# Two-layer hybrid trunk on one core: wider column groups for the sparse attention's projections and the recurrence's values, four split weight pairs, a second set of banks for one FFN product

## The chip, the cores and the metric

The kernel runs on one core of a Trainium2 chip. The metric is the device time of one launch in microseconds (us). Three runs of the kernel before took 2005.44, 2006.55 and 2009.55 us; the median is 2006.55 us.

## The reference

The program is two layers of a decoder trunk for 512 tokens of width 1024, all in float32. The reference, cut to its lines that matter:

```python
h = rmsnorm(x, norm_mix)
(a_x, a_b, a_c, d_q, d_k, d_v, i_q, i_k, i_w,
 g_q, g_f, g_i, g_g, m_q, gate_logits) = split_cols(h @ w_in)
y_a = a_b * causal_conv3(a_c * a_x, conv_w)                 # A: gated convolution
# B: sparse attention: index scores, the 128 highest per token, softmax over these
rel = relu(einsum('bthd,bsd->bths', iq, ik) * idx_scale)
score = where(causal, einsum('bths,bth->bts', rel, iw), -inf)
_, sel = lax.top_k(score, topk)
p = softmax(where(valid, einsum('bthd,btkd->bthk', q, k[sel]) * att_scale, -inf))
y_b = einsum('bthk,btkd->bthd', p, v[sel])
o_c = hgrn2_chunkwise(silu(g_q), -expm1(log_f), g_i, log_f) # C: gated recurrence, values g_i
y_c = rmsnorm(o_c, hgrn_out_norm) * silu(g_g)
y_m = softmax(mq @ mk * scale) @ mv                         # M: attention into 256 memory tokens
merged = sum(gates[:, :, n] * (branches[n] @ w_lift[n]) for n in range(4))
x = x + merged @ w_out
hf = rmsnorm(x, norm_ffn)
gate, up = split(hf @ ffn_w_up, 2)
x = x + (silu(gate) * up) @ ffn_w_down
```

## The kernel before, in words

Every large product is done on TensorE in three float32 passes. An operand is split into a rounded part and a remainder (`_hi` and `_lo`), and `mm3` issues hi·hi, lo·hi and hi·lo for each 128-deep step of the contraction: lines L298, L299 and L300. A weight piece is loaded raw by SP's queue (L253; two raw buffers of 2048 columns), and split 1024 columns at a time: ScalarE writes `w_hi` (L118, the line of the helper through which all its operations go), VectorE writes `w_lo` (L262). A split pair is one such `w_hi` with its `w_lo`; there are `W_BUFS` = 3 of them, and a pair is free again when the last product has read it. `tc.high_priority(offset=AHEAD)` puts these splits ahead of other work.

With `features` the weight tile is what TensorE holds and h is streamed, always 512 columns. With `tokens` the h tile is held and the weights are streamed: the product is as wide as the piece of weights. `tokens` is used at two places:

- `projections` computes what sparse attention needs, for the columns of k, v, the index queries and key, and q: five pieces of 256, 256, 200, 256 and 256 columns, each of all eight contraction steps, and for each piece the four token tiles of 128. A handler (`c_kv`, `c_iq`, `c_last`, `c_q`) empties the accumulation bank: `unit` copies heads out with ScalarE, `headnorm` and `rope` follow, and `heads_T` transposes them.
- `values` computes the recurrence's values g_i as two pieces of 256 columns.

The order on each engine is made when the program is built: a list scheduler walks the instructions in the order of the code, with the priorities above, and keeps a modelled time. In the code, `script(EARLY[l], ...)` takes turns between four generators, by a string of letters: b is one piece of `projections`, c the convolution, m the memory branch, s a step of the top-k selection (8 highest by L881, replaced by L882, repeated). What is left of the selection is woven with `lift(3)` (the product of branch M with `w_lift`). Then `lift(0)` and `values` are woven with the attention itself, `attend`: per query tile and group of four heads, `dots` (L742, L743) into a bank `at`, an addition of the bias with a minimum on VectorE (L755, tile `prob`), the exponential, a reciprocal (L758) and the scaling, four transposes to a bank `tr` (L766), a copy `pt` by ScalarE, and the product with the values `vt` (L772). The recurrence follows. Its `logits` fill accumulation banks `mm` with `features`, and VectorE takes each of them out into a tile `zf`, `zq` or `zg` (L937). Those tiles take the memory of the attention's `prob` and `pt`. There are three banks `mm`, three `tr` and two `at`.

The memory branch reads its keys `mk` and values `mv` back from `kv`, an array in HBM that the start of the program writes; these loads (L664, L688) are in SP's queue between the loads of weights.

In the FFN seven products of blocks (`p1` to `p7`) form `A`, `B` and `C` in PSUM, and VectorE adds them up in tiles `merged` (`plus`, L1319). For the last column group q, `p4` accumulates anew in the banks `B`, after `plus(e, e, B)` has read them.

Of the kernel before, what the change touches and what calls it, by code (L numbers as in the profile page):

```python
# [41 lines left out]
NONC = -2.0e38  # L42
OFF = -1.0e30
AHEAD = 3000
EARLY = ["mmbcmmbmmbsccsmmcsssmsccbmb", "mmbmmbmmcbsccsmmcsssmsccbmb"]
MM_BUFS = 3
TR_BUFS = 3
AT_BUFS = 2
# [1 line left out]
HG = ["zzzHHlHlHzzzHHHHll", "zzzHHHHllzzzHHHllH"]  # L50
WARM, FILL = 9, 5
LOOK = ["0000", "0010"]
W_BUFS, RAW_BUFS, G_BUFS, PT_BUFS, PR_BUFS = 3, 2, 4, 2, 5
MV_BUFS, MP_BUFS = 1, 3
SPACER = 48
R1, R2 = 6, 3
# [14 lines left out]
def hybrid_trunk(ctx: ExitStack, tc: tile.TileContext, x, mem, positions, norm_mix, w_in, conv_w,  # L71
# [38 lines left out]
    def A(dst, src, func, **kw):  # L110
        names = tables.get(func, ())
        name = table["set"] if table["set"] in names else next(iter(names), None)
        if name is not None and name != table["set"]:
            load = act.preload_act_table_set(name)
            for u in table["users"]:
                tc.add_manual_dep(load.ins, u.name, order, reason="table set")
            table.update(set=name, load=load.ins, users=[])
        i = act.activation(dst, src, func, **kw)  # L118
        if name is not None:
            tc.add_manual_dep(i.ins, table["load"].name, order, reason="table set")  # L120
            table["users"].append(i.ins)
        return i

    def mm_ps():
        return bank["mm"]()
# [148 lines left out]
    def wchunk(src, kt, n):  # L274
        return Chunk(src, kt, n)

    def pair(a, k, s=slice(None)):
        return a[0][:, k, s], a[1][:, k, s]
# [8 lines left out]
                    mm3(ps, w.tile(k, j), pair(a, k0 + k), k0 + k == 0, k0 + k == kt - 1)  # L287
        return pss

    def tokens(w, a, t, ps, k0=0, kt=None):  # L290
        kt = w.kt if kt is None else kt
        for k in range(k0, k0 + w.kt):
            mm3(ps, pair(a, k, slice(t * P, (t + 1) * P)), w.at(k - k0), k == 0, k == kt - 1)

    def mm3(ps, a, b, first, last, go_on=False):
        ah, al = a
        bh, bl = b
        pe.matmul(ps, ah, bh, start=first, stop=False, skip_group_check=go_on)  # L298
        pe.matmul(ps, ah, bl, start=False, stop=False, skip_group_check=go_on)  # L299
        pe.matmul(ps, al, bh, start=False, stop=last, skip_group_check=go_on)  # L300
# [249 lines left out]
    def mixer(l, h, norms, cm, cf):  # L550
# [171 lines left out]
                        yield  # L722

        def values(hv):
            for q in range(2):
                w = wchunk(w_in[l][:, C_GI + q * 256:C_GI + (q + 1) * 256], KD, 256)
                for t in range(NT):
                    ps = mm_ps()[:, :256]
                    tokens(w, h, t, ps)
                    A(hv[:, t, q * 256:(q + 1) * 256], ps, AF.Copy, scale=r_t[:, t:t + 1])  # L730
                yield

        with pool_("dsa") as dp:
            qS = dp.tile([P, 8, S], F32R, name="qS")
# [45 lines left out]
            with pool_("idx") as ip:  # L780
# [39 lines left out]
                def unit(ps, t, c0, heads):  # L820
                    u = ip.tile([P, 4, HD], F32, name="unit", bufs=3)[:, :heads]
                    A(u.rearrange("p a b -> p (a b)"), ps[:, c0:c0 + heads * HD], AF.Copy, scale=r_t[:, t:t + 1])
                    return u
# [11 lines left out]
                    A(dst[0][:, s], ps, AF.Copy)  # L835
                    dve.tensor_sub(dst[1][0:HD, s], ps[0:HD], f(dst[0][0:HD, s]))

                def iq_part(ps, t, c0, heads, h0):
                    u = unit(ps, t, c0, heads)
                    rope(u, heads, t)  # L840
                    heads_T(iqS, h0, u.rearrange("p a b -> p (a b)"), heads, t)

                def c_kv(ps, t):
                    A(vt[:, t, :], ps[:, 64:128], AF.Copy, scale=r_t[:, t:t + 1])
                    twin(ps, t, 0, True, kS)
                    iq_part(ps, t, 128, 2, 0)

                def c_iq(ps, t):
                    iq_part(ps, t, 0, 4, 2)

                def c_last(ps, t):
                    A(iw[:, t, :], ps[:, 192:200], AF.Copy, scale=r8_t[:, t:t + 1])
                    iq_part(ps, t, 0, 2, 6)
                    twin(ps, t, 128, False, ikS)

                def c_q(q):
                    def go(ps, t):
                        u = unit(ps, t, 0, 4)
# [3 lines left out]
                    return go  # L862

                def select(t):
                    n = (t + 1) * P
# [19 lines left out]
                    dve.tensor_scalar(biases[t], score, REPL, OFF, op0=OP.not_equal, op1=OP.mult)  # L885

                def projections():
                    for c0, n, handle in ((C_DK, 256, c_kv), (C_DK + 256, 256, c_iq), (C_DK + 512, 200, c_last),
                                          (C_DQ, 256, c_q(0)), (C_DQ + 256, 256, c_q(1))):
                        w = wchunk(w_in[l][:, c0:c0 + n], KD, n)  # L890
                        for t in range(NT):
                            ps = mm_ps()[:, :n]
                            tokens(w, h, t, ps)
                            handle(ps, t)
                        yield

# [284 lines left out]
    def ffn(l, h, sx, ssq, xr, spare, late):  # L1181
# [9 lines left out]
        with tc.tile_pool(name="ffn", bufs=1) as fp:  # L1191
# [44 lines left out]
            def accs(name):  # L1236
                return [bank[name]() for _ in range(2)]
# [14 lines left out]
            def p5(q):  # L1252
                d = st[q]
                d["C"] = accs("C")
                product(d["C"], S1, d["X"].split(), True)
# [26 lines left out]
                product(st[q]["B"], S3, st[q]["Y"].split(), False)  # L1282

            def p4(q):
                product(st[q]["B"], A22, st[q]["X"].split(), False)

            def silu_mul(dst, src, t, other):
                A(dst, src, AF.Silu, scale=norm["r"][:, t:t + 1])
# [33 lines left out]
            for q in range(Q):  # L1322
                n = widths[q]
                d1, e, u, g = (tmps(i, n) for i in ((0, 1, 2, 3) if q % 2 else (3, 1, 2, 0)))
                p1(q, flush)
                d = st[q]
                if q == 0:
                    p5(0)
                    late()
                    r = norm_token(ssq)  # L1330
                    nr = small(NT, name="nrstd_t", bufs=2)
                    dve.tensor_scalar(nr, r, -1.0, None, op0=OP.mult)
                    norm.update(r=r, n=nr)
                with hi_prio():
                    for t in range(2):
                        A(d1[t], d["A"][t][:, :n], AF.Copy)
                plus(e, d1, d["C"], n)
                p6(q)
                plus(u, d1, d["B"], n)
                p3(q)  # L1340
                if q + 1 < Q:
                    first_sum(q + 1)
                plus(u, u, d["C"], n)
                p2(q)
                for t in range(2):
                    silu_mul(g[t], d["A"][t][:, :n], t, u[t])
                p7(q)
                plus(e, e, d["B"], n)
                turn(g, 0, q)
                if q + 1 < Q:  # L1350
                    p5(q + 1)
                p4(q)
                plus(d1, d1, d["B"], n)
                for t in range(2):
                    silu_mul(d1[t], d1[t], t + 2, e[t])
                pending.append((d1, 2, q))
                if q in ends:
                    flush()
                    res = down(q)
# [40 lines left out]
```

## Time and profile before

| what | value |
|---|---|
| median of three runs | 2006.55 us |
| the profiled execution's own time | 2013.66 us |
| its span, first to last instruction | 2012.0 us |
| TensorE matmuls (PE), busy share of the span | 99% |
| TensorE weight loads (PEld) | 84% |
| VectorE (DVE) | 69% |
| ScalarE (ACT) | 51% |
| mean granted TensorE clock | 0.997 |

The profile is of one execution; the span leaves out 1.66 us before the first and after the last instruction. The busy share of an engine is an average over all stages. A duration in the timeline is that of one instruction from its start to its modelled end; TensorE overlaps consecutive matmuls, so that the time which one adds is the distance between two starts. The idle time in front of an instruction stands in brackets, with what ended it.

### The profile page before, as it was taken

How to read it: one execution, taken by the hardware profiler on the slowest of the kernel's cores; microseconds unless marked ns; L12 is line 12 of the kernel's file. 1: busy time of each engine (PE TensorE's matmuls, PEld its weight loads, DVE VectorE, ACT ScalarE, POOL GpSimd, SP SyncE). 2: the span in 40 equal slices, each digit the busy share in tenths (PEclk: the TensorE clock that was granted, in tenths of full speed). 3: DMA queues.
4: the chain of work that ended last, by engine and by line, in shares of the span. 5: the costliest groups of instructions: out<-in, count | busy, mean ns of one | idle time of the engine just before them, and what ended most of it. 6: DMA issues, size and time to landing. Idle time of an engine off the chain costs nothing. (4 is left out here: it accounts for less than half of the span.)

```text
span 2012.0 us, 26848 instructions
## 1 busy us (share of the span) xinstructions
PE 1999.4 (99%) x10249; PEld 1685.9 (84%) x10249; DVE 1391.2 (69%) x2649; ACT 1034.6 (51%) x1797; POOL 69.6 (3%) x85
## 2 busy tenths in 40 slices
PE   9999999999999999999999999999999999999999
PEld 7898988888888888888889898878888888888887
DVE  6679998547666788458657889853687577863772
ACT  7554543766564655325445455366666455532551
POOL 1000000000000010000000000000000000100100
PEclk9999999999999999999999999999999999999999
DMA  8623233222224376354342313331222446644442
GB/s 280 198 82 105 69 95 95 63 64 84 84 84 147 105 199 168 105 136 105 110 157 90 95 58 95 95 95 42 86 83 73 136 122 172 167 126 126 107 113 94
DMA packets 174548, 226.89 MB, mean 113 GB/s; under 512 B 5954, under 2 KB 124308, under 8 KB 174420
## 3 DMA queue, kind: packets, MB, share of 16 engines
q1 hardware_dynamic: 157120, 193.55, 30.3%
q0 software_dynamic: 13344, 23.21, 7.0%
q10 hardware_dynamic: 3956, 8.42, 1.1%
q8 instruction: 81, 1.33, 0.3%
q14 instruction: 47, 0.39, 0.1%
HBM read 214.67 MB, written 10.49 MB: 112 GB/s over the span
## 5 line engine op out<-in xcount | busy, mean ns | idle before, releaser
L118 ACT ACTIVATE w_hi<-w_raw 128x1024 fp32r<-128x1024 f32 (+1 forms) x362 | 373.4, 1033 | 470.7 <-PE mm L299 153.4
L262 DVE TENSOR_TENSOR w_lo<-w_raw,w_hi 128x1024 fp32r<-128x1024 f32 x258 | 311.9, 1210 | 216.2 <-ACT w_hi L118 210.5
L298 PE MATMUL mm<-h_hi,w_hi 128*128 128x512 f32 x960 | 378.8, 396 | 0.6 <-ACT w_hi L118 0.6
L299 PE MATMUL mm<-h_lo,w_hi 128*128 128x512 f32 x960 | 376.8, 393 | 0.0
L300 PE MATMUL mm<-h_hi,w_lo 128*128 128x512 f32 x960 | 374.3, 391 | 0.0
L298 PEld LDWEIGHTS mm<-h_hi,w_hi 128*128 128x128 f32 x960 | 180.4, 188 | 38.0 <-issue 1.7
L300 PEld LDWEIGHTS mm<-h_hi,w_lo 128*128 128x128 f32 x960 | 180.4, 188 | 36.9 <-issue 0.5
L299 PEld LDWEIGHTS mm<-h_lo,w_hi 128*128 128x128 f32 x960 | 180.5, 188 | 36.6 <-issue 1.4
L1177 DVE TENSOR_TENSOR w_lo<-w_raw,w_hi 128x1024 fp32r<-128x1024 f32 (+1 forms) x104 | 117.9, 1142 | 52.6 <-ACT w_hi L118 52.4
L299 PE MATMUL mm<-w_lo,h_hi 128*128 128x256 f32 (+1 forms) x448 | 128.9, 288 | 0.0
L300 PE MATMUL mm<-w_hi,h_lo 128*128 128x256 f32 (+1 forms) x448 | 128.6, 287 | 0.0
L298 PE MATMUL mm<-w_hi,h_hi 128*128 128x256 f32 (+1 forms) x448 | 127.4, 286 | 0.0
L300 PE MATMUL mm<-y_hi,w_lo 128*128 128x512 f32 x256 | 101.3, 396 | 0.0
L299 PE MATMUL mm<-y_lo,w_hi 128*128 128x512 f32 x256 | 100.5, 393 | 0.0
L298 PE MATMUL mm<-y_hi,w_hi 128*128 128x512 f32 x256 | 100.2, 393 | 0.0
L118 ACT ACTIVATE w_hi<-f_raw 128x1024 fp32r<-128x1024 f32 (+1 forms) x64 | 62.7, 979 | 66.4 <-PE B L300 38.6
L299 PEld LDWEIGHTS mm<-w_lo,h_hi 128*128 128x128 f32 x448 | 86.6, 193 | 2.2 <-issue 1.5
L300 PEld LDWEIGHTS mm<-w_hi,h_lo 128*128 128x128 f32 x448 | 86.6, 193 | 1.4 <-issue 0.8
L298 PEld LDWEIGHTS mm<-w_hi,h_hi 128*128 128x128 f32 x448 | 86.3, 194 | 0.5
L118 ACT ACTIVATE prob<-prob,small 128x128 f32<-128x128 f32 (+3 forms) x128 | 69.0, 556 | 32.1 <-DVE small L755 25.0
L1177 DVE TENSOR_TENSOR w_lo<-f_raw,w_hi 128x1024 fp32r<-128x1024 f32 (+1 forms) x64 | 71.7, 1122 | 17.1 <-ACT w_hi L118 17.0
L299 PE MATMUL B<-w_lo,s_hi 128*128 128x512 f32 (+1 forms) x192 | 71.7, 375 | 0.2 <-DVE w_lo L1177 0.2
(438 smaller groups left out, 4350.3 us busy)
## 6 DMA issues: line engine op xcount, KB each, us to landing
w_raw<-in_w_in_dram SPq DMA_DIRECT2D x72, 1024.0 KB, 5.2
w_raw<-in_ffn_w_up_dram SPq DMA_DIRECT2D x60, 512.0 KB, 4.8
w_raw<-in_ffn_w_down_dram SPq DMA_DIRECT2D x18, 1024.0 KB, 5.4
w_raw<-in_w_lift_dram SPq DMA_DIRECT2D x32, 512.0 KB, 3.4
w_raw<-in_ffn_w_up_dram POOLq DMA_DIRECT2D x24, 512.0 KB, 6.3
f_raw<-in_ffn_w_up_dram SPq DMA_DIRECT2D x20, 512.0 KB, 5.0
w_raw<-in_w_out_dram SPq DMA_DIRECT2D x8, 1024.0 KB, 5.3
f_raw<-in_ffn_w_up_dram POOLq DMA_DIRECT2D x16, 512.0 KB, 8.6
```

The costliest lines, as they stand in the source:

```text
L118: i = act.activation(dst, src, func, **kw)
L262: dve.tensor_sub(lo, raw[:, k:e], f(hi))
L298: pe.matmul(ps, ah, bh, start=first, stop=False, skip_group_check=go_on)
L299: pe.matmul(ps, ah, bl, start=False, stop=False, skip_group_check=go_on)
L300: pe.matmul(ps, al, bh, start=False, stop=last, skip_group_check=go_on)
L1177: dve.tensor_sub(lo, self.raw[:, 2 * i:2 * i + 2, :], f(hi))
```

## The change

`projections` takes its columns in three groups of 512, 200 and 512, and `values` in one of 512. A new function `halves` loads a group of 512 as two raw pieces of four contraction steps each, which are four split pairs; `tokens` walks over both pieces for one token tile before it goes to the next. `W_BUFS` becomes 4, and the memory for the fourth pair comes from a smaller scratch for DMA descriptors (`dynamic_dma_scratch_size=4096`). The handlers first copy all heads out of the bank, and then go on with them. The strings `EARLY` have three b instead of five. In the FFN the last `p4` accumulates in banks `C`, and `plus` for the earlier content of `B` stands ahead of it.

```diff
-EARLY = ["mmbcmmbmmbsccsmmcsssmsccbmb", "mmbmmbmmcbsccsmmcsssmsccbmb"]
+EARLY = ["mmbcmmmmbsccsmmcsssmsccbm", "mmbmmmmcbsccsmmcsssmsccbm"]
-W_BUFS, RAW_BUFS, G_BUFS, PT_BUFS, PR_BUFS = 3, 2, 4, 2, 5
+W_BUFS, RAW_BUFS, G_BUFS, PT_BUFS, PR_BUFS = 4, 2, 4, 2, 5
-    def tokens(w, a, t, ps, k0=0, kt=None):
-        kt = w.kt if kt is None else kt
-        for k in range(k0, k0 + w.kt):
-            mm3(ps, pair(a, k, slice(t * P, (t + 1) * P)), w.at(k - k0), k == 0, k == kt - 1)
+    def halves(src, n):
+        per = min(KD, 2048 // n)
+        return [(k0, wchunk(src[k0 * P:(k0 + per) * P], per, n)) for k0 in range(0, KD, per)]
+
+    def tokens(ws, a, t, ps):
+        for k0, w in ws:
+            for k in range(k0, k0 + w.kt):
+                mm3(ps, pair(a, k, slice(t * P, (t + 1) * P)), w.at(k - k0), k == 0, k == KD - 1)
         def values(hv):
-            for q in range(2):
-                w = wchunk(w_in[l][:, C_GI + q * 256:C_GI + (q + 1) * 256], KD, 256)
-                for t in range(NT):
-                    ps = mm_ps()[:, :256]
-                    tokens(w, h, t, ps)
-                    A(hv[:, t, q * 256:(q + 1) * 256], ps, AF.Copy, scale=r_t[:, t:t + 1])
-                yield
+            ws = halves(w_in[l][:, C_GI:C_GI + 512], 512)
+            for t in range(NT):
+                ps = mm_ps()
+                tokens(ws, h, t, ps)
+                A(hv[:, t, :], ps, AF.Copy, scale=r_t[:, t:t + 1])
+            yield
                 def c_kv(ps, t):
                     A(vt[:, t, :], ps[:, 64:128], AF.Copy, scale=r_t[:, t:t + 1])
+                    u0, u1 = unit(ps, t, 128, 2), unit(ps, t, 256, 4)
                     twin(ps, t, 0, True, kS)
-                    iq_part(ps, t, 128, 2, 0)
+                    iq_part(u0, t, 0)
+                    iq_part(u1, t, 2)
...
-                    for c0, n, handle in ((C_DK, 256, c_kv), (C_DK + 256, 256, c_iq), (C_DK + 512, 200, c_last),
-                                          (C_DQ, 256, c_q(0)), (C_DQ + 256, 256, c_q(1))):
-                        w = wchunk(w_in[l][:, c0:c0 + n], KD, n)
+                    for c0, n, handle in ((C_DK, 512, c_kv), (C_DK + 512, 200, c_last), (C_DQ, 512, c_q)):
+                        ws = halves(w_in[l][:, c0:c0 + n], n)
             def p4(q):
-                product(st[q]["B"], A22, st[q]["X"].split(), False)
+                d = st[q]
+                if q == Q - 1:
+                    d["C"] = accs("C")
+                product(d["BC"[q == Q - 1]], A22, d["X"].split(), q == Q - 1)
...
+                if q + 1 == Q:
+                    plus(d1, d1, d["B"], n)
                 p4(q)
-                plus(d1, d1, d["B"], n)
+                plus(d1, d1, d["BC"[q + 1 == Q]], n)
...
-    nc = _bacc.Bacc("TRN2", target_bir_lowering=False, num_devices=1)
+    nc = _bacc.Bacc("TRN2", target_bir_lowering=False, num_devices=1, dynamic_dma_scratch_size=4096)
```

Three places where the order moves are shown. The first is SP's queue at the first piece of `projections` in layer 0. `w_raw` are pieces of weights (8x256 is a piece of eight contraction steps of 256 columns), `mk` and `mv` the keys and values read back from `kv0`. Before:

```order
L253 DMA w_raw_973<-in_w_in_dram 128x8x256
L253 DMA w_raw_1253<-in_w_in_dram 128x8x256
L253 DMA w_raw_1391<-in_w_in_dram 128x8x256
L664 DMA mk_837<-kv0 128x512
L664 DMA mk_839<-kv0 128x512
L688 DMA mv_935<-kv0 128x512
```

The same place after the change:

```order
L253 DMA w_raw_973<-in_w_in_dram 128x4x512
L253 DMA w_raw_983<-in_w_in_dram 128x4x512
L253 DMA w_raw_1323<-in_w_in_dram 128x8x256
L253 DMA w_raw_1497<-in_w_in_dram 128x8x256
L668 DMA mk_837<-kv0 128x512
L668 DMA mk_839<-kv0 128x512
```

One more load of weights stands in front of the first `mk`, and the first wide group is two loads.

The second place is TensorE at the end of layer 0's attention: `tr<-ident,prob` are transposes of the probabilities, `tr<-pt,vt` products with the values, `mm<-w,h` belong to `values` (h held), and `mm<-h,w` to the recurrence's `logits`. Before, the last products of the attention stand among both:

```order
L298 MATMUL mm<-w_hi,h_hi 128x256
L766 MATMUL tr<-ident,prob 128x128 x4
L772 MATMUL tr<-pt,vt 64x256 x6
L299 MATMUL mm<-w_lo,h_hi 128x256
L300 MATMUL mm<-w_hi,h_lo 128x256
L298 MATMUL mm<-w_hi,h_hi 128x256
L299 MATMUL mm<-w_lo,h_hi 128x256
L300 MATMUL mm<-w_hi,h_lo 128x256
L298 MATMUL mm<-h_hi,w_hi 128x512
L299 MATMUL mm<-h_lo,w_hi 128x512
L300 MATMUL mm<-h_hi,w_lo 128x512
```

After the change:

```order
L769 MATMUL tr<-ident,prob 128x128
L745 MATMUL at<-k_hi,qS 128x512
L746 MATMUL at<-k_lo,qS 128x512
L775 MATMUL tr<-pt,vt 64x256 x2
L769 MATMUL tr<-ident,prob 128x128 x15
L775 MATMUL tr<-pt,vt 64x256 x8
L302 MATMUL mm<-h_hi,w_hi 128x512
L303 MATMUL mm<-h_lo,w_hi 128x512
L304 MATMUL mm<-h_hi,w_lo 128x512
```

From the last `dots` (L745, L746) to the end of the attention no product of another branch stands between; before there were 73 matmuls of `values` and `logits` between the same `dots` and the attention's last two products.

The third place is VectorE there, after the change, with the buffer numbers: `mm_4454`, `mm_4455` and `mm_4518` are the three accumulation banks, filled by `logits` ahead of the rows above, and the row L302 above is the first of a fourth bank's worth.

```order
L758 ISA prob_4161,small_4162<-at_4158,bias3_809 128x512
L758 ISA small_4162 128x1
L780 TENSOR_TENSOR y_lo_3378<-tr_4117,y_hi_3377 128x2x128
L761 RECIPROCAL small_4163<-small_4163 128x1
L938 TENSOR_TENSOR zf_4504<-mm_4454,rstd_521 128x512
L938 TENSOR_TENSOR zf_4506<-mm_4455,rstd_521 128x512
L938 TENSOR_TENSOR zq_4568<-mm_4518,rstd_521 128x512
```

All three banks are emptied behind the attention's last reciprocal, the first by the row `zf_4504`, which writes into memory that the attention's `prob` and `pt` had. Before, the matmuls of `values` stood in that stretch, and their banks are emptied into a tile with memory of its own.

## Rows read from the trace of the kernel before

**Rows 1.** The page's first part: busy time, share of the span, instructions.
```profile
PE 1999.4 (99%) x10249; PEld 1685.9 (84%) x10249; DVE 1391.2 (69%) x2649; ACT 1034.6 (51%) x1797; POOL 69.6 (3%) x85
```
**Rows 2.** The waits of TensorE: line, releaser, total us, times, longest us.
```profile
PE at L298 <- DMA mk<-kv: 2.0, 1, 2.0
PE mm L298 <- ACT w_hi L118: 1.7, 2, 1.1
...
PE B L298 <- DVE merged L1319: 1.0, 2, 0.5
```
**Rows 3.** Groups by shape on PE: count, busy us, mean ns, idle before.
```profile
L299 PE MATMUL mm<-w_lo,h_hi 128*128 128x256 f32 x384 | 111.2, 290 | 0.0
L300 PE MATMUL mm<-w_hi,h_lo 128*128 128x256 f32 x384 | 110.7, 289 | 0.0
L298 PE MATMUL mm<-w_hi,h_hi 128*128 128x256 f32 x384 | 109.7, 288 | 0.0
```
**Rows 4.** Timeline of PE, 256 columns: start us, duration us, instruction.
```profile
92.01 0.28 PE L298 MATMUL mm<-w_hi,h_hi 128*128 128x256 f32 x1
...
94.53 0.28 PE L298 MATMUL mm<-w_hi,h_hi 128*128 128x256 f32 x1
```
**Rows 5.** Timeline of PE, 512 columns, in the FFN of layer 0.
```profile
859.92 0.39 PE L298 MATMUL A<-a_hi,w_hi 128*128 128x512 f32 x1
...
865.82 0.39 PE L300 MATMUL A<-a_hi,w_lo 128*128 128x512 f32 x1
```
**Rows 6.** Timeline of PE at the first product with the memory's keys.
```profile
78.84 1.05 PE L677 MATMUL tr<-ones_h,sq 128*128 128x1 f32 x8 [0.33 <-ACT sq L118]
81.86 0.38 PE L298 MATMUL at<-mk,qg_hi 128*128 128x256 f32 x1 [1.96 <-DMA mk<-kv]
```
**Rows 7.** Windows behind it: busy us (count) of each engine, granted clock, DMA.
```profile
83.40:90.20 6.80, 6.80 (x34) 6.80 (x33) 1.72 (x10) 3.03 (x13) 0.52 (x1) 0.51 0.05 18
90.20:94.60 4.40, 4.40 (x39) 4.40 (x38) 2.41 (x17) 3.02 (x12) 0.00 (x0) 1.00 0.00 0
```
**Rows 8.** Timeline of SP's DMA issues there.
```profile
73.41 0.37 SPq L253 DMA_DIRECT2D w_raw<-in_w_in_dram  x1
74.00 1.86 SPq L664 DMA_DIRECT2D mk<-kv  x2
```
**Rows 9.** Timeline of DVE there: the split that frees the slot.
```profile
76.12 1.23 DVE L262 TENSOR_TENSOR w_lo<-w_raw,w_hi 128x1024 fp32r<-128x1024 f32 x1 [1.02 <-ACT w_hi L118]
```
**Rows 10.** Timeline of PE at the last p4 of layers 0 and 1.
```profile
978.24 0.36 PE L298 MATMUL B<-w_hi,h_hi 128*128 128x256 f32 x1 [0.52 <-DVE merged L1319]
...
1950.27 0.36 PE L298 MATMUL B<-w_hi,h_hi 128*128 128x256 f32 x1 [0.52 <-DVE merged L1319]
```
**Rows 11.** The page's fifth part, the weight splits on ACT and DVE.
```profile
L118 ACT ACTIVATE w_hi<-w_raw 128x1024 fp32r<-128x1024 f32 (+1 forms) x362 | 373.4, 1033 | 470.7 <-PE mm L299 153.4
L262 DVE TENSOR_TENSOR w_lo<-w_raw,w_hi 128x1024 fp32r<-128x1024 f32 x258 | 311.9, 1210 | 216.2 <-ACT w_hi L118 210.5
```
**Rows 12.** Windows of layer 0's selection and attention, columns as in rows 7.
```profile
150.00:200.00 50.00, 50.00 (x241) 41.73 (x240) 45.32 (x109) 21.16 (x43) 0.21 (x2) 1.00 0.34 106
...
400.00:450.00 50.00, 50.00 (x327) 41.84 (x326) 19.48 (x40) 30.77 (x57) 1.49 (x4) 1.00 0.21 64
```
**Rows 13.** Timeline of PE, the last attention group of layer 0.
```profile
420.19 0.50 PE L742 MATMUL at<-k_hi,qS 128*128 128x512 f32 x1
...
429.00 0.60 PE L766 MATMUL tr<-ident,prob 128*128 128x128 f32 x4
429.53 1.52 PE L772 MATMUL tr<-pt,vt 128*64 128x256 f32 x12
```
**Rows 14.** Timeline of ACT, the same group.
```profile
422.73 0.72 ACT L118 ACTIVATE prob<-prob,small 128x512 f32<-128x512 f32 x1 [0.23 <-DVE small L758]
...
426.11 1.57 ACT L118 ACTIVATE pt<-tr 128x512 f32<-128x512 f32 x3 [2.29 <-PE tr L766]
```
**Rows 15.** Timeline of DVE, the first bank of logits.
```profile
440.87 0.69 DVE L937 TENSOR_TENSOR zf<-mm,rstd 128x512 f32<-128x512 f32 x1 [0.63 <-PE mm L300]
```

More of the change, by code (lines that the diff above doesn't have):

```diff
@@ L836, in twin, with iq_part @@
                     dve.tensor_sub(dst[1][0:HD, s], ps[0:HD], f(dst[0][0:HD, s]))
-                def iq_part(ps, t, c0, heads, h0):
-                    u = unit(ps, t, c0, heads)
+                def iq_part(u, t, h0):
+                    heads = u.shape[1]
                     rope(u, heads, t)
@@ L844, in c_kv, with c_q @@
                     A(vt[:, t, :], ps[:, 64:128], AF.Copy, scale=r_t[:, t:t + 1])
+                    u0, u1 = unit(ps, t, 128, 2), unit(ps, t, 256, 4)
                     twin(ps, t, 0, True, kS)
-                    iq_part(ps, t, 128, 2, 0)
-                def c_iq(ps, t):
-                    iq_part(ps, t, 0, 4, 2)
+                    iq_part(u0, t, 0)
+                    iq_part(u1, t, 2)
                 def c_last(ps, t):
                     A(iw[:, t, :], ps[:, 192:200], AF.Copy, scale=r8_t[:, t:t + 1])
-                    iq_part(ps, t, 0, 2, 6)
+                    u0 = unit(ps, t, 0, 2)
                     twin(ps, t, 128, False, ikS)
-                def c_q(q):
-                    def go(ps, t):
-                        u = unit(ps, t, 0, 4)
+                    iq_part(u0, t, 6)
+                def c_q(ps, t):
+                    us = [unit(ps, t, q * 256, 4) for q in range(2)]
+                    for q, u in enumerate(us):
                         headnorm(u, 4, gq_b[l])
@@ L861, in go @@
                         heads_T(qS, 4 * q, u.rearrange("p a b -> p (a b)"), 4, t)
-                    return go
                 def select(t):
@@ L887, in projections @@
                 def projections():
-                    for c0, n, handle in ((C_DK, 256, c_kv), (C_DK + 256, 256, c_iq), (C_DK + 512, 200, c_last),
-                                          (C_DQ, 256, c_q(0)), (C_DQ + 256, 256, c_q(1))):
-                        w = wchunk(w_in[l][:, c0:c0 + n], KD, n)
+                    for c0, n, handle in ((C_DK, 512, c_kv), (C_DK + 512, 200, c_last), (C_DQ, 512, c_q)):
+                        ws = halves(w_in[l][:, c0:c0 + n], n)
                         for t in range(NT):
                             ps = mm_ps()[:, :n]
-                            tokens(w, h, t, ps)
+                            tokens(ws, h, t, ps)
                             handle(ps, t)
```

## The prediction

> **What bounds the kernel now.** I read the page's first part before anything else: TensorE is busy for 99% of the span, VectorE for 69%, ScalarE for 51% [rows 1]. Then the waits of TensorE, to see whether the 1% is worth having: the longest is 2.0 us, before the first product with the memory's keys, and the two before the last `p4` add up to 1.0 us; what else there is stays under 2 us a line [rows 2]. So the kernel is a dense stream of matmuls, and the time changes in three ways only: by what a matmul costs, by a wait that goes, by a wait that comes. For the third I went through the order of the changed program on TensorE and looked for places where it has nothing else to do, then priced these from the timeline of before. All sums are made against the profiled execution, 2013.66 us (span 2012.0 and 1.66 around it), and carried over to the median of the runs, 2006.55, by adding the same difference.
>
> **Width.** The pieces that become 512 wide are 1152 matmuls of 256 columns over both layers (three lines of 384, [rows 3]): per layer 4 of the 5 pieces of projections and both of the values, 6 pieces x 4 token tiles x 8 steps x 3 passes = 576. They become 576 of 512 columns. The mean of 290 ns in rows 3 is not their price, since neighbours overlap; the distance of starts is. From 92.01 to 94.53 there are 21 steps in 2.52 us: 120 ns [rows 4]. From 859.92 to 865.82 there are 26 steps in 5.90 us: 227 ns [rows 5]. So 1152 x 0.120 = 138.2 us become 576 x 0.227 = 130.8 us: **-7.5 us**. All of it is on the path, as PE is what bounds. The piece of 200 columns stays.
>
> The Trainium skill ("TensorE: Matmul & The Clock Gate", section "Back-to-back issue gap") gives N/2.4 + 2.5 ns for an isolated matmul of N columns at the fast clock; it says itself that this leaves out the weight loads at small N. By that formula a pair of 256 would cost 218.4 ns against 215.8, and the change would be worth 576 x 2.6 ns = 1.5 us. The trace differs, 240 against 227, and the measurement decides.
>
> **The last `p4`.** It has banks of its own, so the wait of 0.52 us in each layer goes [rows 10]; the matmul behind the gap also takes longer to get going (0.36 us where its neighbours take 0.28), which makes about 0.6 us each: **-1.2 us**. The additional `plus` ahead of it lies on VectorE beside p4's matmuls. Bounds: 0 (the banks C come as late) to -1.4.
>
> **The start.** TensorE waits 1.96 us for `mk`, after a stretch of eight matmuls of one column [rows 6], and then runs 6.80 us with a granted clock of 0.51 before it is back at 1.00 [rows 7]: at 0.51 that stretch does 3.5 us of work, so it loses about 3.3 us. Together 5.3 us hang on this load. It was issued at 74.00 [rows 8] and landed at 81.86. In the changed order one more load of weights stands in SP's queue ahead of it, and that one waits for a raw buffer, that is for the split which before stood at 76.12 and ended at 77.35 [rows 9]. So `mk` is issued at about 78.0 and lands 7.9 us later, at 85.9. TensorE also comes later: ahead of the product the new order has 43 matmuls of the projections' first group, 512 wide, 43 x 0.227 = 9.8 us, where 24 of 256 stood, 2.9 us. It came there at 79.90 (81.86 less the wait), so now 6.9 us later, at 86.8, or a little before, since one matmul of another kind has moved behind it. That is less than 1 us after the load. If it waits 2 us again nothing is gained, if it doesn't wait 5.3 are. I take **-3.5**, two thirds of the way to no wait, for a lead of under 1 us is not safe.
>
> **The splits.** A group of 512 wants four pairs for its first token tile. A pair is a ScalarE split of 1.03 us and a VectorE split of 1.21 us [rows 11], which overlap. The first pair of the next group is free when the last token tile has done its first two steps, 18 matmuls x 0.227 = 4.1 us ahead of the group's end, and needs 2.2 us; the fourth is free only at the group's end, and is wanted 18 x 0.227 = 4.1 us later against the same 2.2. So there are 1.9 us in hand each time, as long as the splits aren't queued behind other work; VectorE is 45.32 of 50 us busy during the selection [rows 12], but the splits have priority over it. I take 0; the other end is 1 us for each of six groups, +6. The handlers' copies move from one bank of 256 to one of 512 with the same work: 0.
>
> **The attention's end.** Here something comes. VectorE bounds the selection [rows 12], so the attention doesn't move up with TensorE's work: in the new order more of `lift(0)` and of the values stands ahead of the first `dots`, and less is left beside the last ones. Behind the last `dots` of a layer before there are 73 matmuls of values and logits; now there are only transposes (15) and products with `vt` (10), and then a logits matmul whose bank must first be emptied by `zf`. That VectorE operation stands behind the attention, for its memory is that of `prob` and `pt`. So TensorE runs through the attention's chain with empty hands:
>
> Last `dots` at 0 (before: 420.19, [rows 13]); minimum, exponential and reciprocal until the scaling starts at 2.54, which ends at 3.26 (before: 422.73 and 0.72 us, [rows 14]). Then the transposes, 0.3 to the first bank; four copies `pt` on ScalarE, of which three took 1.57 us [rows 14], so 2.1; the last products, 0.13 each (12 in 1.52 us, [rows 13]) and the hop to VectorE, 0.4 together; `zf`, 0.69 [rows 15]; the next matmul. That makes 6.9 us. TensorE's own work in it is 0.5 for the dots, 15 transposes at 0.11 (four are 0.60 from the first start to the last end [rows 13], which is three steps and a last duration much like the 0.28 of rows 4) and 10 products at 0.13, together 3.4 us. So it is idle for 3.5 us; if ScalarE still has two scalings of neighbouring heads (0.72 each) in front, 4.9. I take 4.5 in each of two layers: **+9 us**. In the trace of before the same chain took from 420.19 to beyond 429.53, and no row of the waits has it, because the values' matmuls covered it.
>
> **The sum:** -7.5 - 1.2 - 3.5 + 9.0 = -3.2, so 2010.5 in the profile and 2003.4 in the median; I say 2003.5.
>
> **The rivals.**
>
> 1. *The tails are covered.* TensorE reaches the attention's end later than I think (it runs the real order with waits that I can't see), so that `zf` is through when it is wanted; for it speaks that before shows no wait on any operation of the attention, although its transposes stood just as close behind their copies. Against it, the order has no filler there. Then -7.5 - 1.2 - 3.5 = -12.2, and with half a wait left in one layer -10: 1994.5 to 1997.
>
> 2. *The clock falls at the tails: slower.* The only long gap of the trace, 1.96 us, was followed by 6.80 us at 0.51 [rows 6, 7], 1.2 instead of 2.4 GHz. The tails' gaps are longer, with transposes and short products between them. If the clock falls after each of them, at 3.3 us apiece, and the wait is 5.0 each, the tails cost 16.6 instead of 9.0: -12.2 + 16.6 = +4.4, 2011.0. It decides as soon as a tail's wait exceeds the 1.96 us by which the clock fell at the start and stays unbroken; for one tail alone it is +0.1 to +0.6, 2007. Against it: the waits are split into pieces by transposes and products.
>
> 3. *The width is worth only its columns.* If the 120 ns of rows 4 hold only where I read them and elsewhere a 256 costs half a 512, 113.5 ns [rows 5], the first term is 0 and the time 2011; with the skill's formula it is 2009.5. Against it: the same 0.28 and 0.29 us of duration in rows 3 over all 1152.
>
> 4. *Splits of four pairs are late*, one us for each of six groups: +2.8, 2009.4.
>
> 5. *The change doesn't do what it says*: `p4` waits for the banks C instead and `mk` is as late as before: 3.5 + 1.2 are not gained, 2008.
>
> **Chances.** Forecast as summed, with its own range of 2001 to 2006: 0.40. Rival 1: 0.22. Rival 2 with both tails 0.10, with one tail 0.10. Rival 3: 0.03, rival 4: 0.08, rival 5: 0.07. What a measurement of this kernel can tell from no change is 0.2%, 4.0 us: faster is below 2002.5, slower above 2010.6. Faster: all of rival 1, and of the forecast the two fifths in which the start gains its full 5.3 or the tails cost 3.5: 0.22 + 0.16 = 0.38. Slower: of rival 2 with both tails and of rival 3 about two thirds, and a part of rivals 4 and 5 together with a lost start, 0.09 + 0.08 = 0.17. Within: 0.45. The range for 8 in 10 cuts rival 1's best tenth and the worst of rival 2: 1995 to 2012.
>
> **What would show it.** Right: the distance of starts 0.227 us in projections and values; no row of the waits for `merged` L1319 at p4; two waits of TensorE of 3 to 5 us in total at the end of the attention, around 415 to 430 and 1355 to 1370 us, on `zf`, on ScalarE's `pt` or on `prob`; in the windows behind them a granted clock of 1.00. Wrong: PE idle in the projections on `w_hi` or `w_lo` (rival 4), a window at 0.5 behind the attention (rival 2), no wait there at all (rival 1), and `mk` with 2 us again (part of rival 5). The forecast fails above all if the tail's chain is hidden, or is much longer than 5 us a layer.

## The result and the profile after

The changed kernel takes 2026.78 us (four runs, 2024.76 to 2028.42), the kernel before beside it 2007.72 us: a ratio of 1.0095, 95% interval 1.0078 to 1.0113. It is 19.1 us slower. The prediction said 2003.5 us, with a range of 1995 to 2012, and gave slower a chance of 0.17. It was wrong.

The profiled execution took 2027.79 us, 14.1 more than that of before. The two figures differ because the profiled run of before (2013.66) is one of its longer ones: it has the wait for `mk` and the half clock behind it [rows 6, 7], some 5.5 us together, and a kernel with the same start has less of it (0.2 us of wait in the one with `p4` alone, below). So the medians are explained with the start left out.

The first part of the page after the change, which answers to [rows 1]:

```profile
PE 1998.3 (99%) x9673; PEld 1654.5 (82%) x9673; DVE 1389.4 (69%) x2653; ACT 1029.6 (51%) x1789; POOL 69.9 (3%) x85
```

TensorE is busy for 1.1 us less, not 7.5, and its idle time has grown from 12.6 to 27.7 us. The mean granted clock is 0.997 in both, so it is not half clock that takes the rest of the 7.5; the busy time counts late starts without a gap too, and the *excess* below holds both. The waits of TensorE (line, releaser, total, times, longest) answer to [rows 2]. `gate` is the tile into which VectorE empties a bank of `lift`'s gates; `mprob` are the memory branch's probabilities, `mpt_hi` the copy of their transposes, `qg_hi` and `qg_lo` the two parts of its queries.

```profile
PE mm L302 <- DVE gate L575: 6.4, 4, 2.4
PE mm L302 <- DVE qg_lo L678: 3.2, 3, 1.6
PE at L302 <- ACT mpt_hi L118: 2.6, 2, 1.4
PE C L302 <- DVE merged L1323: 2.0, 2, 1.6
PE tr L769 <- ACT prob L118: 1.9, 4, 0.6
PE mm L302 <- DVE zf L938: 1.7, 2, 0.9
```

None of the first four is in the list of before, and of the six only the last two groups (`prob`, `zf`) are at the place that the prediction named.

**What came as forecast.** The width: one group of the three of `tokens` (count, busy, mean ns, as in [rows 3]), and the timeline of a wide group, first and last of 18 starts without a gap:

```profile
L303 PE MATMUL mm<-w_lo,h_hi 128*128 128x512 f32 x192 | 75.1, 393 | 0.0
```

```profile
90.10 0.39 PE L302 MATMUL mm<-w_hi,h_hi 128*128 128x512 f32 x1
...
93.96 0.39 PE L304 MATMUL mm<-w_hi,h_lo 128*128 128x512 f32 x1
```

17 steps in 3.86 us are 0.227 each, and three lines of 192 are the 576. The start: SP's issue of `mk`, TensorE's first product with it, and the granted clock behind that (columns as in [rows 7]) answer to [rows 6 to 8]:

```profile
77.04 1.52 SPq L668 DMA_DIRECT2D mk<-kv  x2
```

```profile
85.29 0.95 PE L681 MATMUL tr<-ones_h,sq 128*128 128x1 f32 x8
86.10 0.37 PE L302 MATMUL at<-mk,qg_hi 128*128 128x256 f32 x1
```

```profile
86.00:90.00 4.00, 4.00 (x23) 3.47 (x23) 1.36 (x8) 2.54 (x10) 0.00 (x0) 1.00 0.00 0
```

`mk` goes out 3.0 us later and the product starts 4.2 us later, without a wait, and the clock stays at 1.00.

**What was not forecast: the memory branch.** Beside the projections, TensorE stops in both layers. First the windows of TensorE, before and after (busy, count, granted clock, DMA), then its timeline, that of ScalarE, and a window of all engines (busy of PE, PEld, DVE, ACT, POOL, granted clock, DMA), all three after:

```profile
100.00:150.00 50.00, 50.00 (x356) 1.00 0.29 87
100.00:150.00 50.00, 47.31 (x280) 0.97 0.38 117
```

```profile
138.11 0.70 PE L714 MATMUL tr<-ident,mprob 128*128 128x128 f32 x4 [0.33 <-DVE mprob L712]
140.06 0.58 PE L302 MATMUL at<-mpt_hi,mv 128*128 128x256 f32 x1 [1.25 <-ACT mpt_hi L118]
...
143.76 0.50 PE L302 MATMUL mm<-h_hi,w_hi 128*128 128x512 f32 x1 [0.77 <-DVE qg_lo L678]
```

```profile
137.37 2.00 ACT L118 ACTIVATE w_hi<-w_raw 128x1024 fp32r<-128x1024 f32 x2
139.26 0.26 ACT L118 ACTIVATE iw<-mm,r_t 128x8 f32<-128x8 f32 x1
139.41 0.59 ACT L118 ACTIVATE mpt_hi<-tr 128x512 fp32r<-128x512 f32 x1
```

```profile
137.00:144.00 7.00, 4.65 (x24) 3.89 (x24) 5.65 (x10) 5.16 (x12) 0.00 (x0) 0.76 0.40 118
```

The chain probabilities, transposes, copy, product with `mv` has nothing between its steps any more; the copy `mpt_hi` stands behind two weight splits on ScalarE, and TensorE waits through it, and then runs at the lower of its two levels, 1.2 GHz (granted clock 0.50 from 140.2 to 143.4 us, 0.76 over the window). In layer 1 the same comes at 1117 to 1122 us, at full clock, and one more wait before it. A window of PE, then PE, ACT and DVE at that earlier wait:

```profile
1080.00:1124.00 44.00, 39.95 (x244) 1.00 0.40 124
```

```profile
1087.13 0.50 PE L302 MATMUL mm<-h_hi,w_hi 128*128 128x512 f32 x1 [1.61 <-DVE qg_lo L678]
```

```profile
1085.11 0.69 ACT L118 ACTIVATE qg_hi<-mm,prm 128x512 fp32r<-128x512 f32 x1 [4.79 <-PE mm L304]
...
1086.49 0.47 ACT L118 ACTIVATE unit<-mm,rstd_t 128x256 f32<-128x256 f32 x1
```

```profile
1086.32 0.75 DVE L678 SCALAR_TENSOR_TENSOR qg_lo<-mm,prm,qg_hi 128x512 fp32r<-128x512 f32 x1 [3.15 <-ACT sq L118]
```

ScalarE's order has `qg_hi` ahead of the `unit` copies of a wide tile; it sits idle 4.79 us for `qg_hi`'s bank, and the `unit` copies behind it come after it. No run shows whether they could have come sooner: their buffers are read by transposes that start at 1085.02.

**What was not forecast: the selection.** At the wide q group TensorE first waits for a rotated unit and then for a bank that VectorE has not emptied; PE, then DVE:

```profile
257.88 0.41 PE L814 MATMUL tr<-ident,unit 128*128 128x128 f32 x2 [0.28 <-DVE unit L799]
260.69 0.50 PE L302 MATMUL mm<-h_hi,w_hi 128*128 128x512 f32 x1 [2.40 <-DVE gate L575]
```

```profile
257.65 0.42 DVE L808 TENSOR_TENSOR unit<-unit,small 128x256 f32<-128x256 f32 x1
257.99 0.55 DVE L883 MAX8 m<-score 128x8 f32<-128x384 f32 x1
...
259.08 0.43 DVE L809 TENSOR_TENSOR unit<-unit,gq 128x256 f32<-128x256 f32 x1
...
259.95 0.68 DVE L575 TENSOR_TENSOR gate<-mm,rstd 128x512 f32<-128x512 f32 x1
```

VectorE has no gap there, while TensorE does 20.25 us in a window of 24 (columns: busy, count, granted clock, DMA). Before, it had no gap there; its window stands first:

```profile
250.00:300.00 50.00, 50.00 (x227) 1.00 0.29 89
250.00:274.00 24.00, 20.25 (x96) 1.00 0.20 65
```

The bank is emptied by `gate` at 259.95, behind q's normalization and the selection.

**The attention's end**, as forecast in kind; PE and then DVE, which answer to [rows 13, 15]:

```profile
446.46 0.55 PE L769 MATMUL tr<-ident,prob 128*128 128x128 f32 x3 [0.64 <-ACT prob L118]
447.48 1.12 PE L769 MATMUL tr<-ident,prob 128*128 128x128 f32 x4 [0.47 <-ACT pt L118]
448.53 2.99 PE L775 MATMUL tr<-pt,vt 128*64 128x256 f32 x16
452.38 0.50 PE L302 MATMUL mm<-h_hi,w_hi 128*128 128x512 f32 x1 [0.87 <-DVE zf L938]
```

```profile
451.64 1.29 DVE L938 TENSOR_TENSOR zf<-mm,rstd 128x512 f32<-128x512 f32 x2 [5.98 <-PE tr L775]
```

**Where the time went, by stage.** For each matmul I take the distance from its start to the next start and subtract its price (0.227 us for 512 columns, 0.178 for 384, 0.120 for 256, 0.112 for 200, 0.110 for 128, and so on); the sum over a stage is its *excess*. It holds waits and half clock alike; half clock behind the new waits is three stretches after the change (granted clock 0.50 from 140.2, 447.4 and 1239.2 us), some 1.7 us each. In us, layer 0 / layer 1:

| kernel | memory branch | selection | attention's end |
|---|---|---|---|
| before | 3.5 (the start's half clock) / 0.3 | 0.4 / 0.4 | 3.8 / 3.9 |
| after | 5.3 / 5.6 | 5.7 / 6.3 | 7.7 / 6.1 |
| e1 turns at half groups | 3.3 / 1.6 | 10.8 / 9.9 (half clock in both) | 4.9 / 3.7 |
| e2 order only, 256 wide | 4.4 (the start's half clock) / 0.4 | 2.8 / 2.3 | 3.3 / 3.3 |
| e3 values 256 wide | 6.8 / 5.6 | 5.2 / 5.3 | 5.3 / 5.3 |
| e5 q 256 wide | 6.9 / 5.6 | 3.9 / 3.9 | 5.0 / 4.9 |
| e6 first group 256 wide | 1.7 (the start's half clock) / 0.4 | 5.7 / 6.5 | 4.9 / 3.7 |
| e7 all projections 256 wide | 0.2 / 0.4 | 0.5 / 0.3 | 3.6 / 3.5 |
| e8 no normalization of q | 6.9 / 5.6 | 2.5 / 2.4 | 4.3 / 4.2 |
| e12 neither that nor rotation | 6.8 / 5.6 | 2.6 / 2.5 | 5.1 / 5.1 |

The stages are: from the first product with `mk` to the first scoring product; from there to the last scoring product; from the first attention product to the first of the recurrence. Since e7 shows an undisturbed 0.2 for the memory branch of layer 0, the change adds 5.1 + 5.3 there, 5.3 + 5.9 in the selection and 3.9 + 2.2 at the attention's end, 27.7 us; the output projections and the FFNs lose 0.8 and the width 7.5. That is +19.4, against 19.1 in the medians; the spans say 14.0 more and 5.5 at the start of before.

### The profile page after: what moved, and what is told of

It is laid out like the page before. It is cut to its first block, busy times and chain, and to the rows that moved or that the text cites. A ratio compares the mean times of both kernels' runs of the same rounds, so it can differ in the third digit from the quotient of the medians.

```text
span 2026.0 us, 25666 instructions
## 1 busy us (share of the span) xinstructions
PE 1998.3 (99%) x9673; PEld 1654.5 (82%) x9673; DVE 1389.4 (69%) x2653; ACT 1029.6 (51%) x1789; POOL 69.9 (3%) x85
## 3 DMA queue, kind: packets, MB, share of 16 engines
q8 instruction: 76, 1.25, 0.3%
## 5 line engine op out<-in xcount | busy, mean ns | idle before, releaser
L302 PE MATMUL mm<-h_hi,w_hi 128*128 128x512 f32 x960 | 378.4, 395 | 10.4 <-DVE gate L575 4.8
L302 PEld LDWEIGHTS mm<-h_hi,w_hi 128*128 128x128 f32 x960 | 180.7, 188 | 49.5 <-DVE gate L575 5.3
L302 PE MATMUL mm<-y_hi,w_hi 128*128 128x512 f32 x256 | 100.8, 398 | 1.8 <-DVE gate L575 1.6
L304 PE MATMUL mm<-w_hi,h_lo 128*128 128x512 f32 (+1 forms) x256 | 93.6, 367 | 0.0
L303 PE MATMUL mm<-w_lo,h_hi 128*128 128x512 f32 (+1 forms) x256 | 92.9, 364 | 0.0
L302 PE MATMUL mm<-w_hi,h_hi 128*128 128x512 f32 (+1 forms) x256 | 92.5, 364 | 0.0
L1169 DVE TENSOR_TENSOR f_raw<-f_raw,w_raw 128x1024 f32<-128x1024 f32 (+1 forms) x40 | 44.7, 1116 | 39.8 <-DMA w_raw<-in_ffn_w_up_dram 39.5
L304 PE MATMUL B<-w_hi,s_lo 128*128 128x512 f32 (+1 forms) x192 | 71.8, 375 | 0.0
L303 PE MATMUL A<-w_lo,h_hi 128*128 128x512 f32 (+1 forms) x192 | 71.2, 371 | 0.0
```

Of the source, the lines that this page charges most:

```text
L1169: dve.tensor_add(self.raw[:, k, :], self.raw[:, k, :], other.raw[:, k, :])
```

## The experiments

Theory 1 was at first that the turns make the waits, theory 2 that the width does. The short diffs are against the changed kernel where nothing else is said.

**e1_half_turns.**

```diff
-EARLY = ["mmbcmmmmbsccsmmcsssmsccbm", "mmbmmmmcbsccsmmcsssmsccbm"]
+EARLY = ["mmbmmbmmcbsccsmmcsssmsccbmb", "mmbmmbmmcbsccsmmcsssmsccbmb"]
...
                             handle(ps, t)
+                            if n == 512 and t == 1:
+                                yield
```

> The changed kernel, in which a group of 512 columns gives up its turn after two of its four token tiles too, so that the strings again hold five b, those of layer 1 before the change for both layers. Theory 1 (the new waits of TensorE at 137 to 143, 257 to 267, 1085 to 1121 and 1236 to 1247 us come from the turns: memory branch steps follow each other, and the last q group has one step behind it, without products between them): the 21.2 us of excess at these places go, and since 36 to 50 matmuls stand again behind the last dots of the attention, most of its 7.9 us too: 1998 to 2003. Theory 2 (they come from the width: a group holds all four pairs and gives VectorE twice the work at a time): at least 15 of the 21 stay, 2015 to 2025.

2023.28 us, 1.0076 [1.0061, 1.0091]. The time lies in the range of theory 2. Theory 1 holds for the memory branch alone, and there in part: 5.6 fell to 1.6 in layer 1, and 5.3 to 3.3 in layer 0. In the selection it became worse; PE and DVE of this kernel:

```profile
255.03 0.63 PE L714 MATMUL tr<-ident,mprob 128*128 128x128 f32 x4 [4.15 <-DVE mprob L712]
```

```profile
253.90 0.17 DVE L709 RECIPROCAL small<-small 128x2 f32<-128x2 f32 x1
254.00 0.09 DVE L884 MATCH_VALUE_LOAD score<-m,score 128x8 f32 x1
254.07 0.54 DVE L884 MATCH_REPLACE8 score<-m,score 128x384 f32<-128x384 f32 x1
254.53 0.61 DVE L712 TENSOR_SCALAR mprob<-mprob,small 128x256 f32<-128x256 f32 x2
```

A step of the memory branch in the middle of the q group puts TensorE at the mercy of two small VectorE operations that stand behind the selection: 4.15 us in one wait, and half clock behind it, which makes 3.4 of the stage's 10.8. A turn helped here only where the engine that it needs was not behind.

**e2_order_only** (against the kernel before).

```diff
-EARLY = ["mmbcmmbmmbsccsmmcsssmsccbmb", "mmbmmbmmcbsccsmmcsssmsccbmb"]
+EARLY = ["mmbbcmmmmbsccsmmcsssmsccbbm", "mmbbmmmmcbsccsmmcsssmsccbbm"]
```

> The kernel before, 256 wide and with three pairs, with only its turns changed: the two pieces that became one group take their turns one right after the other (bb where the changed kernel has the b of a wide group). Theory 1: the waits of the memory branch and at the end of the turns appear without any wide group, 15 to 22 us slower than before, 2022 to 2029. Theory 2: no wait of TensorE over 1 us there, within 4 us of before.

2014.51 us, 1.0031 [1.002, 1.0043], some 6 us slower: between the two. The memory branch has no excess in layer 1 (0.4), so turns alone don't make that one, and by e1 it is smaller when the turns come back: it takes both; the selection has 2.4 and 1.9 more than before, so turns alone make something over a third of that.

**e3_values_narrow.**

```diff
-            ws = halves(w_in[l][:, C_GI:C_GI + 512], 512)
...
+            for q in range(2):
+                ws = halves(w_in[l][:, C_GI + q * 256:C_GI + (q + 1) * 256], 256)
...
```

> The changed kernel with the recurrence's values again as two pieces of 256. 52 matmuls stand then between the last dots and the end of the attention in each layer. If the attention's tail is a lack of other products there, its 7.9 us go and 2.5 us of width are lost (a third of 7.5): about 5 us faster than the changed kernel, 2021.5. If the tail comes because the whole attention is 20 us later than before, the waits stay and it is 2.5 us slower than the changed kernel, 2029.

2028.05 us, 1.0102 [1.0087, 1.0117]: against my expectation not faster than the changed kernel. The time is that of the second case (2029), but the waits did not stay: the excess at the attention's end fell from 13.8 to 10.6 in sum, 3.2, and 2.5 of width went. The 7.9 that I had expected is what the change adds from the last dots on, and there the excess fell from 8.7 to 2.4; ahead of the last dots it rose by 3.1. Over the whole stage the change adds 6.1, so that the missing matmuls make about half of that.

**e4_p4_only** (against the kernel before): the three hunks on `p4` and `plus` alone.

```diff
...
-                product(st[q]["B"], A22, st[q]["X"].split(), False)
+                product(d["BC"[q == Q - 1]], A22, d["X"].split(), q == Q - 1)
...
```

> The kernel before with only the last p4 in banks C and the additional plus ahead of it. By the prediction's term: no wait for merged L1319 ahead of p4 in either layer, 1.2 us faster than before. Rival: the wait moves to the next user of a bank or to a split, 0.

2007.84 us against 2008.44, 1.0003 [0.9993, 1.0013]. The wait for `merged` L1319 is gone from the list, and the FFNs take 0.6 and 0.5 us less from their first matmul to their last. That is below what the times can tell.

**e5_kv_wide and e6_q_wide**, each with one of the two wide groups of projections taken back, in the turns of before at that place.

```diff
...
-                    for c0, n, handle in ((C_DK, 512, c_kv), (C_DK + 512, 200, c_last), (C_DQ, 512, c_q)):
+                    for c0, n, handle in ((C_DK, 512, c_kv), (C_DK + 512, 200, c_last),
+                                          (C_DQ, 256, c_q(0)), (C_DQ + 256, 256, c_q(1))):
```

> The changed kernel with only the first group of projections and the values 512 wide; q is again two pieces of 256 with a step of the memory branch between them (the last b of the strings before). If each wide group makes the waits at its own place: the 12 us of excess between the first and the last scoring product (both layers) fall below 3, the 11 us between the first memory product and the first scoring product stay; 2.5 us of width are lost: 2012 to 2019. If four pairs as such make the waits, both places keep theirs, 2025 and more.

```diff
...
+                    for c0, n, handle in ((C_DK, 256, c_kv), (C_DK + 256, 256, c_iq), (C_DK + 512, 200, c_last), (C_DQ, 512, c_q)):
```

> The changed kernel with q and the values 512 wide, and the first columns again as two pieces of 256 with two steps of the memory branch between them. Each wide group at its own place: the 11 us at the memory branch go, the 12 us in the selection stay: 2014 to 2021. Four pairs as such: both stay, 2025 and more.

e5: 2021.91 us, 1.0064 [1.0048, 1.0081]; e6: 2016.61 us, 1.0038 [1.0023, 1.0053]. Windows of TensorE at the memory branch and in the selection of layer 0 (busy, count, granted clock, DMA), of e5 and of e6:

```profile
130.00:150.00 20.00, 17.93 (x109) 0.83 0.39 128
250.00:274.00 24.00, 21.49 (x99) 1.00 0.21 66
```

```profile
130.00:150.00 20.00, 20.00 (x164) 1.00 0.25 80
250.00:274.00 24.00, 20.24 (x93) 1.00 0.20 67
```

The memory branch's waits belong to the first wide group: gone in e6, all there in e5. Those of the selection can't be shared out between the two groups: with q alone wide (e6) all of them are there, and with the first group alone wide (e5) 3.9 us are still left in each layer where I expected under 3 in sum. There the first scoring product comes at 164 us, in e7 at 145: the first group puts the selection off as well.

**e7_only_values.** Both taken back, with the strings of before.

> The changed kernel with all projections 256 wide in the turns of before: of the change the values 512 wide, the fourth pair, the smaller scratch and the last p4 are left. Each wide group at its own place: no excess at either place, 2.5 us of width gained and about 0.8 of p4, a wait at the attention's end of at most 2 us a layer as 62 matmuls stand behind the last dots: 1 to 3 us faster than before. Four pairs or the scratch as such: 5 us and more slower than before.

2005.35 us against 2008.15, 0.9988 [0.9978, 0.9997], as expected, and the fastest here. The same windows:

```profile
130.00:150.00 20.00, 20.00 (x162) 1.00 0.29 90
250.00:274.00 24.00, 24.00 (x110) 1.00 0.28 89
```

TensorE has no gap, with the values 512 wide in one turn and four pairs. So neither the four pairs nor the width of the values cost anything at these two places or at the attention's end (3.6 and 3.5).

**e8_no_headnorm and e12_no_norm_rope.** VectorE is relieved at the wide q group, and ScalarE of a square and three short operations for each unit; TensorE's work is the same. In the changed kernel ScalarE sat idle for 2.46 us up to 258.64, where the wait for `gate` begins, and VectorE had no gap.

```diff
...
                     for q, u in enumerate(us):
-                        headnorm(u, 4, gq_b[l])
-                        rope(u, 4, t)
                         heads_T(qS, 4 * q, u.rearrange("p a b -> p (a b)"), 4, t)
```

(e8 takes out the first of the two lines, e12 both.)

> The changed kernel without the normalization of q's heads: eight times 1.56 us of VectorE's work a layer are left out, at the wide q group, and nothing of TensorE's. Theory A (VectorE gets q's work for 512 columns at a time, beside the selection, and falls behind; TensorE waits for banks and transposes that VectorE has yet to reach): the 12 us between the first and the last scoring product fall below 4, about 2017. Theory B (four pairs held by one group leave TensorE no other product to go to): they stay above 9, 2024 to 2027.

> The changed kernel without the normalization and without the rotation of q's heads: besides the 1.56 us a unit another four short VectorE operations of about 0.2 us are left out for each of eight units a layer, and nothing of TensorE's. The excess between the first and the last scoring product was 5.7 and 6.3 us in the changed kernel, 2.5 and 2.4 without the normalization, 0.4 in the kernel before. Theory A (VectorE's backlog): it falls to 1.2 or less in each layer, 2010 to 2013. Theory B (the pairs held by the wide group make what is left): it stays at 2 or more in each layer.

e8: 2014.63 us, 1.0029 [1.0019, 1.0039]; e12: 2017.44 us, 1.0042 [1.0026, 1.0059]. The selection's excess fell from 12.0 to 4.9 in e8, a little above the 4 of theory A, and the wait for `gate` is gone; what is left there is a short one:

```profile
258.66 0.63 PE L714 MATMUL tr<-ident,mprob 128*128 128x128 f32 x4 [0.70 <-DVE mprob L712]
```

In e12 it stayed at 2.6 and 2.5, where theory A wanted 1.2 or less, with one wait of 0.8 us for `gate` in each layer again. So q's normalization makes about 3.5 us a layer (5.7 to 2.5, 6.3 to 2.4), by VectorE's backlog as far as the timeline shows, and the last 2 us a layer don't go with q's work on VectorE. They are as large as what the turns alone made in e2 (2.4 and 1.9), which fits, but no run takes them away with q 512 wide; that the pairs held by a wide group make them is not excluded. Nor are the three buffers of `unit`: the last bank of q is filled at 231.65 us in the changed kernel and free only at 249.33, in e8 8.5 us after it is filled, for each copy into `unit` starts just behind transposes that read an older one. One bank held so long is not enough (15.6 us in e7, without a wait), and no run has more buffers.

**e9_scratch, e10_pairs, e11_scratch_8192.** The first two are the kernel before with the smaller scratch, and with a fourth pair as well; the third is e7 with a scratch of 8192.

```diff
-W_BUFS, RAW_BUFS, G_BUFS, PT_BUFS, PR_BUFS = 3, 2, 4, 2, 5
+W_BUFS, RAW_BUFS, G_BUFS, PT_BUFS, PR_BUFS = 4, 2, 4, 2, 5
...
-    nc = _bacc.Bacc("TRN2", target_bir_lowering=False, num_devices=1)
+    nc = _bacc.Bacc("TRN2", target_bir_lowering=False, num_devices=1, dynamic_dma_scratch_size=4096)
```

> The kernel before with only the smaller scratch for DMA descriptors (4096). The FFN of layer 0 has 2 to 3 us more excess in the changed kernel's kind (values wide, fourth pair, scratch) than before, with TensorE waiting for merged ahead of banks C at 744 to 754 us. If the scratch makes that, by holding back GpSimd's accumulating loads: 2 to 3 us slower than before, with that wait. If the fourth pair does, through the order of loads: the same time as before, no such wait.

> The kernel before with the smaller scratch and the fourth split pair, everything else as before. If the fourth pair makes the FFN's wait: 2 to 3 us slower than before with a wait of 1 to 2 us ahead of banks C in layer 0. If the scratch does, the same as the run with the scratch alone. If both are free: within 1 us of before.

> The fastest version so far (values 512 wide, projections 256 in the old turns, fourth pair, last p4 in banks C) with a scratch of 8192 in place of 4096. If the scratch costs in the FFN, 2 to 3 us faster than that version, 5 us faster than before; if the fourth pair does, the same as that version, 2 to 3 us faster than before.

e9: 0.9999 [0.9989, 1.0008]; e10: 1.0005 [0.9995, 1.0014]; e11: 2006.99 us against 2009.51, 0.9989 [0.998, 0.9998]. The wait ahead of banks C is there in e10 and not in e9, one line of the waits of e10:

```profile
PE C L298 <- DVE merged L1319: 1.4, 2, 1.0
```

So the fourth pair brings it, in a way that no run shows, and the scratch does not (e11 gains nothing over e7 and has 1.7 us of the same wait). In time it is less than can be told.

## Why the prediction was wrong

- **Width, -7.5: right**, the starts are 0.227 us apart and 576 matmuls are there. An estimate by the formula of the Trainium skill for an isolated matmul ("TensorE: Matmul & The Clock Gate", section "Back-to-back issue gap") would have made it 1.5.
- **p4, -1.2: right by itself, not in the whole.** The wait is gone, and in e4 the two FFNs take 1.1 us less. In the changed kernel they take only 0.1 less, since TensorE waits 2.0 us for `merged` ahead of banks C, at an earlier product than the last `p4`, a wait that the fourth pair brings (e10). Another 0.7 went ahead of the second FFN, in the output projection, and e10 has that too.
- **Start, -3.5: right in the profile, of little worth in the medians.** I put the issue of `mk` at 78.0 and TensorE at 86.8; it was 77.04 and 86.10. The wait and the half clock are gone, some 5.5 us against the profiled run of before. But that run was one with an unusually long start, and I carried its loss over to the median as if every run had it.
- **Attention's end, +9: right in mechanism, over-sized.** The waits stand on `prob`, `pt` and `zf`. From the last dots on the excess grew by 7.9 us in the two layers, over the whole stage by 3.9 and 2.2. (The steps of the chain add up to 6.75 us, not 6.9.) It goes by the number of matmuls of other branches behind the last dots, as I had it: a layer has 0.4 us of excess from there on with 73 of them (before), 0.6 with 62 (e7), 1.3 with 50 (e5), 2.0 with 12 (e6, layer 0), 5.1 and 3.6 with none. But the wide values alone don't empty that place: e7 has them. It takes the wide projections ahead of it. They also make the attention start late, at 329 us against 304 in e7, but a late start is not enough: in e5 it is 328, and 50 matmuls are left.
- **The step that failed: "The handlers' copies move from one bank of 256 to one of 512 with the same work: 0" and, with it, the search of the order for places without other work.** I costed the projections' new turns and their emptying at nothing and found only one such place, where there are three in each layer. The memory branch's chain had lost the piece of projection between its steps, and it stands in the order as four steps of the chain side by side, as plainly as the attention's end did. That alone is not the cause: e2 has the same four steps at 256 columns and no waits there in layer 1, so the wide group is part of it, and how it acts there stays open. The memory branch cost 10.4 us in the two layers, the selection 11.2: together 21.6, where the forecast was off by 22.3 (19.1 against -3.2). The start (3.5 us that the medians don't show) and the attention's end (2.9 us less than forecast) nearly cancel.
- **"VectorE bounds the selection" was in my text, and I drew the wrong thing from it.** I let it delay the attention. That an engine that is 45 of 50 us busy [rows 12] also gives back TensorE's banks late, when 512 columns' worth of normalization is put to it at one time, I had written down as "the splits have priority" and let go. e8 puts 3.5 us a layer on it; some 2 us a layer of the selection's waits stay open.
- **The rivals.** None was this one. The slower rival with its 2011 had the half clock at the tail, which came in layer 0 alone (0.87 of full clock from 440 to 453), and at the memory branch (0.76). Its condition, a single wait of over 1.96 us, does not hold: the tail's longest wait was 0.87 us, and the wait of 2.40 us in the selection of layer 0 left the clock at 1.00.

## What to carry over

When a change makes groups of work larger, price not only the work but the turns: list, for every chain that used to have such a group between its steps, what now stands there, and go through all of the chains, not just the one that the eye falls on first. On an engine that is nearly saturated, as VectorE was here (45 of 50 us), a batch of twice the size delays what stands behind it in its order, and among that were the banks of the engine that bounds. Take only the part of a change whose place has slack: here the change without the wide projections and their turns gave 0.12%, and these cost about nine times that (1.0095 against 0.9988).

## What the runs showed that was not expected

- The start of this kernel varies from run to run: TensorE waited for `mk` 2.0, 0.2 and 0.5 us in three kernels with the same work there (before, e4, e9).
- After a stretch with gaps of 0.33 and 1.25 us and four transposes between them, the granted clock was 0.50, its lower level of 1.2 GHz, from 140.2 to 143.4 us; the matmuls of 256 columns then started 0.21 us apart instead of 0.12. A gap of 2.40 us at 258 us did not lower it (1.00 in 250 to 274 us of the kernel after); the gap of 2.40 us at the same place of layer 1 did (0.50 from 1239.2 to 1242.4 us). The length of one gap does not say whether the clock falls.
